# Conv gated MLP in FP32: eight gate tiles begun ahead and kept in DRAM, modulation in single pieces, last six down rows by halves

## Chip, cores and metric

One core of a Trainium2 chip. The metric is the device time of one execution in microseconds; several executions are timed and the median counts. One further execution is profiled. All rows of instructions below come from that one.

## What is computed

An encoder trunk of two layers on x of 1024 tokens by 1024 features, all in FP32. Each layer is a token mixer, which the change leaves alone, and a gated MLP with a convolution of three taps along the tokens. A vector c gives each layer six modulation vectors (shift, scale and gate of both halves).

```python
mod = (c_act @ w_mod[l] + b_mod[l])[:, None, :]
sh1, sc1, g1, sh2, sc2, g2 = jnp.split(mod, 6, axis=-1)
...
x = x + g1 * rms_norm(y, norm_g[l, 1])
h = rms_norm(x, norm_g[l, 2]) * (1 + sc2) + sh2
u = dwconv3(h @ w_up[l], ffn_conv[l])
ug, uv = jnp.split(u, 2, axis=-1)
y = (jax.nn.gelu(ug, approximate=True) * uv) @ w_down[l]
x = x + g2 * rms_norm(y, norm_g[l, 3])
```

D_FF is 2816, so w_up gives 22 tiles of 128 gate features and 22 of values, and w_down has 22 row blocks of 128.

## The kernel before

Features lie on the partitions and tokens along the free dimension, in two halves of 512. Every FP32 product is done as three matmuls on rounded parts, high by high, high by low, low by high; `split` (L110 and L111) makes a part pair from a loaded tile, the high part on ScalarE, the low part on GpSimd or VectorE.

**dense_up** makes one gate tile and its value tile per step t, 22 steps, from seven products of 512 by 512 blocks in place of eight, in the manner of Strassen, 84 matmuls of 128x512 each. `begin` (two quarters with the gate's own weight w1, 24 matmuls) needs token half 0 only; its result goes to u through ScalarE (L1218, L1222). `sums` loads both weights and makes three weight combinations on VectorE (L1238 to L1243); `head` (36 matmuls) and `tail` (24) use these with operands that need both token halves. Five `begin`s run ahead of all, kept in SBUF; the first head is mixed, its matmuls going through the operands one feature block at a time as these become ready. `gated` does the two convolutions (`conv3`, L919 and L921, 128x1024 each on VectorE), the gelu on ScalarE, the product (L1288) and the store to `actd` in DRAM.

**dense_down** walks over the 22 row blocks k. `whole` steps take two or four k, and for each of eight output tiles m run both token halves (48 matmuls per k) and add the result into y on VectorE (L1359, kept as `self.mark`). In layer 0 14 k go so; the last eight, in pairs, go by halves (`some`, 24 matmuls per k and half, adds L1366): first half 0 for all four pairs, then `end(HALVES[0])`, which does norm, residual and the next layer's modulated input for half 0 (lines L143 to L189, L446 to L452, L504, L505), then half 1 and its end. `load_half` is called directly ahead of each pair.

The modulation vectors that later stages need are made beside dense_down. `mod_sum` (L345) loads 16 weight blocks of 128x512; those of the first 512 outputs are multiplied and added up on VectorE (L365, L367), those of the second on ScalarE (L361) and GpSimd (L363). Each of the two series has one buffer. `background` calls it once per step, and a scheduler in the language places the instructions by the priorities that follow from the code's order; loads go on SyncE's queue in that order, and each waits at the head of the queue for its buffer.

Of the kernel before, what the change touches and what calls it, by code (L numbers as in the profile page):

```python
# [92 lines left out]
class Trunk:  # L93
# [251 lines left out]
    def mod_sum(self, l, j, room=None):  # L345

# [513 lines left out]
    def modulations(self):  # L860
# [3 lines left out]
        for j in (2, 4, 3):  # L864
            part = self.mod_sum(0, j, room)
# [50 lines left out]
    def conv3(self, o, t, cw):  # L916
        nc = self.nc
        n = o.shape[1]
        nc.vector.tensor_scalar(o, t[:, 0:n], cw(0), None, op0=ALU.mult)  # L919
# [160 lines left out]
    def mixer(self, l):  # L1080
        tc, nc = self.tc, self.nc
        with ExitStack() as e:
# [28 lines left out]
            self.uctx.close()  # L1111
            self.qlc, kls, rt, self.sc = self.open_shared(f"hmid{l}")
# [73 lines left out]
    def dense_up(self, l, early):  # L1186
# [12 lines left out]
        ahead = 5  # L1199
        with tc.tile_pool(name=f"ux{l}", bufs=4, reuse_waits="tile") as ux, \  # L1200
                tc.tile_pool(name=f"u2{l}", bufs=2, reuse_waits="tile") as u2p, \
                tc.tile_pool(name=f"a2{l}", bufs=1, reuse_waits="tile") as a2p:
            places = cycle(("tc", "tn", "ux", "ux", "ux", "ux"))
# [9 lines left out]
            def begin(w1, between=None):  # L1213

                u = u_tile()
# [3 lines left out]
                if between:  # L1219
                    between(u)  # L1220
                self.quarter(x, w1, 512, b21, False)
                nc.scalar.activation(u[:, c1], x, AF.Copy)  # L1222
                return u
# [24 lines left out]
            def rest(u, w2, w3, w4, uv):  # L1248

                state = {}  # L1250

                def head(u, mixed=False):
                    yb = self.psc.tile([128, 512], F32, name="psc", tag="psc")
                    zw = self.po.tile([128, 1024], F32, name="po", tag="po")
                    z, w = zw[:, 0:512], zw[:, 512:1024]
                    u2 = u2p.tile([128, 512], F32, name="u2", tag="u2")
                    jobs = ((yb, w2, 512, t2), (z, w2, 0, t1), (w, w4, 0, t4))
                    if mixed:
                        for i in range(4):
                            for ps, wx, at, xs in jobs:  # L1260
# [313 lines left out]
```

## Time and profile before

| | us |
|---|---|
| median of 3 runs | 3340.94 (3338.89 to 3341.43) |
| profiled execution | 3335.26 |
| its span | 3333.5 |
| TensorE busy in the span | 2895.6 (87%) |
| VectorE busy | 2380.3 (71%) |
| GpSimd busy | 1244.5 (37%) |
| ScalarE busy | 1167.9 (35%) |
| mean granted TensorE clock | 0.936 |

Times in rows are from the start of the span, which is 1.8 us shorter than the execution. In layer 0 the up projection begins at about 879 us, the down projection at 1374, and layer 1's input is ready at about 1810; in layer 1 the up projection begins at about 2561 and the down projection at 3054. The granted clock is a share of full speed: 1.00 is 2.4 GHz and 0.50 is 1.2 GHz.

### The profile page before, as it was taken

What the parts mean: (1) busy time and instruction counts of PE and PEld (TensorE: products, weight loads), DVE (VectorE), ACT (ScalarE), POOL (GpSimd) and SP (SyncE); (2) the same over time, 40 slices, a digit from 0 to 9 for tenths busy, and PEclk for the clock granted to TensorE, in tenths of its full rate; (3) what the DMA queues carried; (4) which work ended last, traced back from release to release, by engine and by line L of the source; (5) the groups of instructions that cost most, each with busy time, mean ns of one, the idle gap of its engine ahead of it and who ended that gap; (6) DMA issues with size and microseconds to landing.
All of it is one profiled execution on the core that took longest, in us unless ns stands there. A gap on an engine that the chain in (4) does not pass through costs nothing. (4 is left out here: it accounts for less than half of the span.)

```text
span 3333.5 us, 35440 instructions
## 1 busy us (share of the span) xinstructions
PE 2895.6 (87%) x13178; PEld 2296.9 (69%) x13178; DVE 2380.3 (71%) x3203; ACT 1167.9 (35%) x1698; POOL 1244.5 (37%) x853
## 2 busy tenths in 40 slices
PE   7888889988869999997358899889888689999997
PEld 3677667776557888776236787677766478887886
DVE  6686667796579898755485944676976698888456
ACT  4322433553432333322233333435544323333211
POOL 1221223224345545643353221333243454455431
PEclk8998999999979999998679999899999799999999
DMA  5235111012312222444332121101023122223423
GB/s 196 79 106 173 46 33 51 27 44 71 120 45 82 89 76 83 164 161 165 124 125 72 54 82 64 36 27 54 20 89 114 42 91 76 82 88 127 146 89 101
DMA packets 119513, 292.74 MB, mean 88 GB/s; under 512 B 13051, under 2 KB 31739, under 8 KB 119340
## 3 DMA queue, kind: packets, MB, share of 16 engines
q1 hardware_dynamic: 119340, 290.48, 26.4%
q8 instruction: 103, 1.69, 0.2%
q14 instruction: 70, 0.57, 0.1%
HBM read 238.09 MB, written 55.74 MB: 88 GB/s over the span
## 5 line engine op out<-in xcount | busy, mean ns | idle before, releaser
L111 POOL TENSOR_TENSOR wl<-raw,wh 128x1024 fp32r<-128x1024 f32 (+1 forms) x87 | 217.3, 2499 | 462.9 <-ACT wh L110 271.3
L521 PE MATMUL pj<-hh,wh 128*128 128x512 f32 x800 | 328.1, 410 | 12.9 <-DVE ql L570 8.5
L522 PE MATMUL pj<-hl,wh 128*128 128x512 f32 x800 | 322.0, 402 | 1.6 <-POOL hl L450 1.3
L525 PE MATMUL pj<-hh,wl 128*128 128x512 f32 x800 | 209.7, 401 | 0.0
L521 PEld LDWEIGHTS pj<-hh,wh 128*128 128x128 f32 x800 | 154.4, 193 | 53.2 <-issue 15.4
L522 PEld LDWEIGHTS pj<-hl,wh 128*128 128x128 f32 x800 | 154.3, 193 | 36.9 <-issue 2.2
L525 PEld LDWEIGHTS pj<-hh,wl 128*128 128x128 f32 x800 | 152.7, 192 | 36.4 <-issue 1.6
L681 PE MATMUL po<-s,v 128*96 128x128 f32 (+3 forms) x672 | 130.4, 355 | 42.0 <-ACT s L678 41.8
L681 PE MATMUL po<-hp,v 128*96 128x256 f32 x512 | 128.2, 407 | 29.4 <-ACT hp L678 29.0
L110 ACT ACTIVATE wh<-raw 128x1024 fp32r<-128x1024 f32 (+1 forms) x95 | 99.0, 1044 | 146.9 <-PE pj L522 75.6
L681 PEld LDWEIGHTS po<-s,v 128*96 128x96 f32 x672 | 97.9, 185 | 69.7 <-ACT s L678 54.6
L568 ACT ACTIVATE qh<-pj 64x512 fp32r<-64x512 f32 x128 | 107.1, 837 | 98.8 <-PE pj L525 53.3
L570 DVE TENSOR_TENSOR ql<-pj,qh 64x512 fp32r<-64x512 f32 x64 | 55.4, 866 | 115.5 <-ACT qh L568 114.8
L681 PEld LDWEIGHTS po<-hp,v 128*96 128x96 f32 x512 | 87.3, 175 | 64.7 <-ACT hp L678 36.1
L111 POOL TENSOR_TENSOR ul<-raw,uh 128x1024 fp32r<-128x1024 f32 x43 | 112.7, 2621 | 49.5 <-ACT uh L110 49.3
L552 DVE TENSOR_TENSOR ks<-pj,ks 64x512 fp32r<-64x512 f32 x56 | 51.2, 914 | 109.5 <-ACT ks L551 108.9
L921 DVE SCALAR_TENSOR_TENSOR tb<-u,par,tb 128x1024 f32<-128x1024 f32 x88 | 127.0, 1443 | 0.0
L363 POOL TENSOR_TENSOR mc<-mc,mr 128x512 f32<-128x512 f32 x49 | 69.7, 1422 | 152.9 <-ACT mr L361 152.9
L367 DVE SCALAR_TENSOR_TENSOR mc<-mr,cact,mc 128x512 f32<-128x512 f32 x49 | 52.9, 1079 | 100.9 <-DMA mr<-in_w_mod_dram 100.8
L668 PE MATMUL psc<-qh,ks 128*128 128x256 f32 (+2 forms) x272 | 88.5, 339 | 36.4 <-DVE s L796 15.3
L1359 DVE TENSOR_TENSOR y<-y,po 128x1024 f32<-128x1024 f32 x54 | 65.6, 1216 | 68.7 <-PE po L514 68.6
L921 DVE SCALAR_TENSOR_TENSOR ta<-u,par,ta 128x1024 f32<-128x1024 f32 x88 | 114.2, 1297 | 0.0
(562 smaller groups left out, 9126.1 us busy)
## 6 DMA issues: line engine op xcount, KB each, us to landing
mr<-in_w_mod_dram SPq DMA_DIRECT2D x144, 256.0 KB, 3.0
raw<-in_w_up_dram SPq DMA_DIRECT2D x54, 512.0 KB, 3.5
raw<-in_w_in_dram SPq DMA_DIRECT2D x52, 512.0 KB, 3.3
raw<-in_w_down_dram SPq DMA_DIRECT2D x52, 512.0 KB, 3.8
actd<-ta SPq DMA_DIRECT2D x44, 512.0 KB, 2.6
uh<-in_w_up_dram SPq DMA_DIRECT2D x26, 512.0 KB, 3.7
room<-in_w_mod_dram SPq DMA_DIRECT2D x48, 256.0 KB, 3.5
xd<-y SPq DMA_DIRECT2D x48, 256.0 KB, 2.4
```

The lines of the kernel that those rows point to most:

```text
L110: self.nc.scalar.activation(hi, src, AF.Copy)
L111: (eng or self.nc.gpsimd).tensor_sub(lo, src, hi.bitcast(F32))
L363: nc.gpsimd.tensor_add(acc, acc, w)
L521: nc.tensor.matmul(ps, wh[:, ks], self.hh[k][:, hs], start=k == 0, stop=False, skip_group_check=True)
L522: nc.tensor.matmul(ps, wh[:, ks], self.hl[k][:, hs], start=False, stop=False, skip_group_check=True)
L525: nc.tensor.matmul(ps, wl[:, ks], self.hh[k][:, hs], start=False, stop=k == KT - 1, skip_group_check=True)
L568: nc.scalar.activation(self.perm(qh[h][o:o + 64], r)[:, n * half:n * half + n, :], src, AF.Copy)
L570: nc.vector.tensor_sub(lo, src, own.bitcast(F32))
L668: nc.tensor.matmul(ps, ks[:, c], qh[:, q0:q1], start=first, stop=False, skip_group_check=True)
L681: nc.tensor.matmul(o[0:96, co], v(tt, h), s[:, cs], start=co.start // 512 not in seen, stop=False, skip_group_check=True)
L921: nc.vector.scalar_tensor_tensor(o, t[:, i:i + n], cw(i), o, op0=ALU.mult, op1=ALU.add)
L1359: self.mark = nc.vector.tensor_copy(d, p) if first else nc.vector.tensor_add(d, d, p)
```

## The change

Up projection, both layers: eight `begin`s in place of five run ahead; each u is stored to a DRAM tensor `kept` from ScalarE's queue and loaded again on SyncE's when its tile's turn comes. The first two tiles are done side by side in one mixed series of matmuls. The first term of each convolution moves from VectorE to ScalarE, and one of the adds at a tile's end from VectorE to GpSimd.

Modulation: 96 pieces (one load, one VectorE multiply-add) with two buffers, none on ScalarE or GpSimd; layer 0 places three behind each tile t of 8 and up, and one or two behind each output add of the down projection.

Down projection of layer 0: 16 k whole, six by halves; all loads of half 1 stand ahead of half 0's end.

```diff
-    def mod_sum(self, l, j, room=None):
+    def mod_pieces(self, l, j, room=None):
...
-                    w = self.mr.tile([128, 512], F32, name="mr", tag=f"mr{u}")
+                    w = self.mr.tile([128, 512], F32, name="mr", tag="mr")
...
-                if u and not room:
-                    nc.scalar.activation(w if k else acc, w, AF.Copy, scale=s)
-                    if k:
-                        nc.gpsimd.tensor_add(acc, acc, w)
-                elif k == 0:
+                if k == 0:
                     nc.vector.tensor_scalar(acc, w, s, None, op0=ALU.mult)
                 else:
                     nc.vector.scalar_tensor_tensor(acc, w, s, acc, op0=ALU.mult, op1=ALU.add)
+                yield
             accs.append(acc)
         return l, j, accs, 0
+    def modulate(self, jobs):
+        for l, j in jobs:
+            part = yield from self.mod_pieces(l, j)
+            self.mod_fold(part, self.mr.tile([128, 512], F32, name="mr", tag="mr"))
+            yield
+    def advance(self, n):
+        with self.tc.issue_after(self.mark.ins):
+            for _ in range(n):
+                next(self.pieces, None)
...
+        if scalar:
+            nc.scalar.activation(o, t[:, 0:n], AF.Copy, scale=cw(0))
+        else:
+            nc.vector.tensor_scalar(o, t[:, 0:n], cw(0), None, op0=ALU.mult)
...
-        ahead = 5
+        ahead = 8
+        kept = self.kept
...
+                def tail(p):
+                    u, uv = p.u, p.uv
+                    if p.x is None:
+                        self.quarter(p.y, p.w3, 0, t3, False)
+                        nc.vector.tensor_add(uv[:, c1], p.y, u[:, c2])
+                    else:
+                        nc.vector.tensor_add(uv[:, c1], p.x, p.u2)
+                    self.quarter(p.z, p.w3, 512, b22, False)
+                    nc.vector.tensor_add(u[:, c2], p.z, p.u2)
+                    nc.gpsimd.tensor_add(uv[:, c2], uv[:, c2], uv[:, c1])
+                    nc.vector.tensor_add(uv[:, c1], uv[:, c1], p.w)
+                    return u, uv
...
+            for t in range(ahead):
+                u = u_tile()
+                begin(u, early[t] if t < len(early) else self.up_weight(l, t))
+                nc.scalar.dma_start(kept[128 * t:128 * t + 128, :], u[:, 1:1025])
+            def kept_pair(t):
+                ws, u = sums(t, False), u_tile()
+                nc.sync.dma_start(u[:, 1:1025], kept[128 * t:128 * t + 128, :])
+                return Pair(u, ws)
+            two = [kept_pair(t) for t in range(2)]
+            jobs = []
+            for p in two:
+                p.x = self.pj.tile([128, 512], F32, name="pj", tag="pj")
+                jobs += [(p.y, p.w2, 512, t2), (p.z, p.w2, 0, t1), (p.x, p.w3, 0, t3)]
+            jobs.insert(2, two[0].p4)
...
+                if t >= ahead:
+                    self.advance(3)
...
             def whole(ops, first):
                 for m in range(8):
+                    if m:
+                        self.advance(1 if len(ops) < 4 else 2)
...
-                for j, ks in enumerate(final):
-                    some(load_half(ks, HALVES[0], room[j % 2]), HALVES[0], whole_half)
+                for ks in final:
+                    some(load_half(ks, HALVES[0], "ppp"), HALVES[0], part)
+                while next(self.pieces, self) is not self:
+                    pass
                 right.close()
+                rest = [load_half(ks, HALVES[1], names) for ks, names in zip(final, ("wwq", "qqq", "fff"))]
                 end(HALVES[0])()
-                for j, ks in enumerate(final):
-                    some(load_half(ks, HALVES[1], room[j % 2]), HALVES[1], whole_half)
+                for ops in rest:
+                    some(ops, HALVES[1], part)
                 end(HALVES[1])()
```

Three places show what moves. The first is SyncE's queue near the end of layer 0's down projection; `mr` are modulation weights, `raw<-in_w_down` weights of the down projection, `qh`, `ql`, `ph`, `pl` its other operand, `xd` the residual. Before:

```order
L501 DMA raw<-xd 128x2x512
L358 DMA mr<-in_w_mod_dram 128x512 x2
L1168 DMA qh<-actd 128x512
L1168 DMA ql<-actd 128x512
L358 DMA mr<-in_w_mod_dram 128x512 x28
L506 DMA xd<-y 128x512 x2
L116 DMA raw<-in_w_down_dram 128x1024
L506 DMA xd<-y 128x512 x6
L116 DMA raw<-in_w_down_dram 128x1024 x2
L501 DMA x<-xd 128x2x512 x2
```

Now (ten loads stand ahead of two whole operands, thirteen ahead of the last half pairs):

```order
L357 DMA mr<-in_w_mod_dram 128x512 x10
L1188 DMA ql<-actd 128x1024
L1188 DMA wl<-actd 128x1024
L116 DMA raw<-in_w_down_dram 128x1024
L1188 DMA qh<-actd 128x512
L1188 DMA ql<-actd 128x512
L357 DMA mr<-in_w_mod_dram 128x512 x13
L1188 DMA ph<-actd 128x512
L1188 DMA pl<-actd 128x512
L116 DMA raw<-in_w_down_dram 128x1024 x2
L357 DMA mr<-in_w_mod_dram 128x512
L1188 DMA ph<-actd 128x512
```

The row of 28 loads directly ahead of the residual's stores is gone; the loads stand earlier, in rows of 13 and fewer, with operand loads between them.

The second is VectorE (and GpSimd) in one steady tile of the up projection of layer 0. L1268 (now L1280) is the add behind the head, L1288 (L1308) the product, L1238 to L1243 (L1257 to L1262) the next weights' sums, L1275 to L1279 (L1293 to L1299) the adds behind the tail. VectorE before:

```order
L1268 TENSOR_TENSOR u_8132<-psc,u 128x512
L1288 TENSOR_TENSOR ta<-ta,tb 128x1024
L1238 TENSOR_TENSOR wl<-raw 128x512
L1239 TENSOR_TENSOR wl<-wl,wh 128x512
L1242 TENSOR_TENSOR raw<-wh,raw 128x512
L1243 TENSOR_TENSOR raw<-wh,wl 128x512
L1275 TENSOR_TENSOR u<-psc,u 128x512
L1278 TENSOR_TENSOR u<-u 128x512
L1277 TENSOR_TENSOR u<-po,u_8132 128x512
L1279 TENSOR_TENSOR u<-u,po 128x512
L919 TENSOR_SCALAR ta<-u,par 128x1024
L919 TENSOR_SCALAR tb<-u,par 128x1024
```

VectorE now (L360 and L362 are pieces):

```order
L1280 TENSOR_TENSOR u_7907<-psc,u 128x512
L1308 TENSOR_TENSOR ta<-ta,tb 128x1024
L360 TENSOR_SCALAR mc<-mr,cact 128x512
L1258 TENSOR_TENSOR ul<-ul,uh 128x512
L362 SCALAR_TENSOR_TENSOR mc<-mr,cact,mc 128x512
L1261 TENSOR_TENSOR raw<-uh,raw 128x512
L1262 TENSOR_TENSOR raw<-uh,ul 128x512
L362 SCALAR_TENSOR_TENSOR mc<-mr,cact,mc 128x512
L1293 TENSOR_TENSOR u<-psc,u 128x512
L1297 TENSOR_TENSOR u<-po,u_7907 128x512
L1299 TENSOR_TENSOR u<-u,po 128x512
L1257 TENSOR_TENSOR wl<-raw 128x512
```

GpSimd now, with the moved add L1298 at its place:

```order
L111 TENSOR_TENSOR vl<-raw,vh 128x512
L111 TENSOR_TENSOR ul<-ul,uh 128x1024
L111 TENSOR_TENSOR wl<-raw,wh 128x1024
L1298 TENSOR_TENSOR u<-u 128x512
```

The pieces stand behind the product and among the sums; both L919 and the add L1278 are gone from VectorE, and the moved add stands on GpSimd behind the splits of the next weights.

The third is ScalarE at the start of the up projection in layer 0, where the operands of token half 1 are prepared (`hx`, `hp`, `t4`, `y` are such operands, `u<-pj` the evacuations of begins). Before:

```order
L110 ACTIVATE t4_6553<-t_6538 128x512
L110 ACTIVATE y_6550<-x_6536 128x512
L110 ACTIVATE y_6556<-sq_6537 128x512
L1218 ACTIVATE u_6635<-pj_6638 128x512
L1218 ACTIVATE u_6671<-pj_6674 128x512
L110 ACTIVATE vh_6746<-raw_6740 128x512
L110 ACTIVATE uh_6744<-raw_6740 128x1024
L1222 ACTIVATE u_6635<-pj_6638 128x512
```

Now:

```order
L110 ACTIVATE t4_6560<-t_6545 128x512
L110 ACTIVATE y_6557<-x_6543 128x512
L110 ACTIVATE y_6563<-sq_6544 128x512
L1238 ACTIVATE u_6638<-pj_6647 128x512
L1238 ACTIVATE u_6675<-pj_6684 128x512
L110 ACTIVATE vh_6869<-raw_6863 128x512
L110 ACTIVATE uh_6826<-raw_6828 128x1024
L1242 ACTIVATE u_6638<-pj_6647 128x512
L1315 DMA kept_86<-u_6638 128x1024
```

The first evacuation of begin 3 (`u_6635`, now `u_6638`) stands behind the last prepared operand in both; the stores to `kept` are new.

## Rows read from the trace of the kernel before

**Rows 1.** Stretches; columns: us, busy (instructions) by engine, TensorE clock, DMA share, GB/s.

```profile
879.00:947.00 68.00, 39.10 (x111) 21.44 (x110) 49.54 (x71) 25.13 (x42) 30.93 (x19) 0.76 0.15 54
947.00:1080.00 133.00, 121.52 (x488) 97.02 (x487) 108.02 (x102) 37.67 (x48) 64.54 (x58) 0.93 0.24 79
1080.00:1374.00 294.00, 294.00 (x1278) 239.92 (x1277) 257.44 (x239) 96.10 (x123) 155.28 (x113) 1.00 0.24 84
1374.00:1608.00 234.00, 206.72 (x863) 164.34 (x861) 142.27 (x180) 66.70 (x82) 116.00 (x63) 0.95 0.52 175
1608.00:1690.00 82.00, 2.90 (x6) 0.88 (x4) 38.24 (x72) 13.58 (x20) 22.43 (x15) 0.52 0.31 101
3054.00:3314.00 260.00, 249.40 (x1168) 208.49 (x1167) 148.96 (x177) 58.44 (x72) 92.40 (x43) 0.98 0.34 117
```

**Rows 2.** TensorE's timeline: start us, us, line, operation [idle before it <-what ended that].

```profile
1608.47 0.39 PE L514 MATMUL pd<-ql 128*128 128x512 f32 x1
...
1690.36 0.80 PE L512 MATMUL pd<-qh,wh 128*128 128x512 f32 x1 [69.92 <-ACT wh L110]
```

**Rows 3.** SyncE's timeline, end of the down projection in layer 0.

```profile
1600.93 69.44 SPq L358 DMA_DIRECT2D mr<-in_w_mod_dram  x28
...
1684.83 0.45 SPq L116 DMA_DIRECT2D raw<-in_w_down_dram  x1
```

**Rows 4.** VectorE's line L367: what ended its idle time, us, times.

```profile
  DMA mr<-in_w_mod_dram: 100.8, 42
```

**Rows 5.** VectorE's timeline between the layers, the two half chains.

```profile
1680.07 0.71 DVE L143 STREAM_TRANSPOSE ta<-sm 128x512 f32<-128x512 f32 x1
...
1730.82 0.74 DVE L452 SCALAR_TENSOR_TENSOR hl<-tc,mod,hh 128x512 fp32r<-128x512 f32 x1
...
1757.41 0.69 DVE L1366 TENSOR_TENSOR y<-y,pd 128x512 f32<-128x512 f32 x1 [0.68 <-PE pd L514]
...
1767.71 0.71 DVE L143 STREAM_TRANSPOSE acc<-sm 128x512 f32<-128x512 f32 x1
...
1807.14 0.75 DVE L452 SCALAR_TENSOR_TENSOR hl<-t,mod,hh 128x512 fp32r<-128x512 f32 x1
```

**Rows 6.** TensorE's timeline, start of the up projection in layer 0.

```profile
929.74 0.80 PE L1263 MATMUL psc<-y,uh 128*128 128x512 f32 x1 [5.75 <-ACT y L110]
```

**Rows 7.** ScalarE's timeline, the same place.

```profile
945.11 0.58 ACT L1218 ACTIVATE u<-pj 128x512 f32<-128x512 f32 x1
```

**Rows 8.** VectorE's groups, 1080 to 1374 us: count | busy us, mean ns | idle.

```profile
L1278 DVE TENSOR_TENSOR u<-u 128x512 f32<-128x512 f32 x16 | 25.9, 1621 | 1.7
L919 DVE TENSOR_SCALAR tb<-u,par 128x1024 f32<-128x1024 f32 x15 | 24.0, 1601 | 0.0
...
L919 DVE TENSOR_SCALAR ta<-u,par 128x1024 f32<-128x1024 f32 x15 | 20.9, 1391 | 0.0
...
L1275 DVE TENSOR_TENSOR u<-psc,u 128x512 f32<-128x512 f32 x16 | 11.1, 692 | 23.3 <-PE psc L1184 23.3
```

**Rows 9.** Two of the page's costliest groups; columns as in rows 8.

```profile
L110 ACT ACTIVATE wh<-raw 128x1024 fp32r<-128x1024 f32 (+1 forms) x95 | 99.0, 1044 | 146.9 <-PE pj L522 75.6
...
L363 POOL TENSOR_TENSOR mc<-mc,mr 128x512 f32<-128x512 f32 x49 | 69.7, 1422 | 152.9 <-ACT mr L361 152.9
```

**Rows 10.** The page's DMA issues: count, KB each, us from issue to landing.

```profile
mr<-in_w_mod_dram SPq DMA_DIRECT2D x144, 256.0 KB, 3.0
raw<-in_w_up_dram SPq DMA_DIRECT2D x54, 512.0 KB, 3.5
...
actd<-ta SPq DMA_DIRECT2D x44, 512.0 KB, 2.6
```

**Rows 11.** VectorE's groups, 1374 to 1608 us; columns as in rows 8.

```profile
L367 DVE SCALAR_TENSOR_TENSOR mc<-mr,cact,mc 128x512 f32<-128x512 f32 x30 | 33.3, 1111 | 61.0 <-DMA mr<-in_w_mod_dram 60.9
```

**Rows 12.** VectorE's timeline, one steady tile of the up projection.

```profile
1161.81 0.68 DVE L1279 TENSOR_TENSOR u<-u,po 128x512 f32<-128x512 f32 x1
```

**Rows 13.** GpSimd's timeline, the same tile.

```profile
1159.33 2.85 POOL L111 TENSOR_TENSOR ul<-raw,uh 128x1024 fp32r<-128x1024 f32 x1
```

More of the change, by code (lines that the diff above doesn't have):

```diff
@@ L864, in modulations @@
         for j in (2, 4, 3):
-            part = self.mod_sum(0, j, room)
+            pieces = self.mod_pieces(0, j, room)
+            try:
+                while True:
+                    next(pieces)
+            except StopIteration as done:
+                part = done.value
             yield
@@ L1211, in u_tile, with begin @@
                 return u
[L1213 to L1215 removed]
+            def begin(u, w1, between=None):
                 x = self.pj.tile([128, 512], F32, name="pj", tag="pj")
@@ L1285, in gated @@
                     base = _P["fconv"] + l * 132 + m
-                    self.conv3(o, u, lambda i: self.par[:, base + 44 * i:base + 44 * i + 1])
+                    self.conv3(o, u, lambda i: self.par[:, base + 44 * i:base + 44 * i + 1], True)
                 nc.scalar.activation(cv[0], cv[0], AF.Gelu_apprx_tanh)
-                nc.vector.tensor_mul(cv[0], cv[0], cv[1])
+                self.mark = nc.vector.tensor_mul(cv[0], cv[0], cv[1])
                 nc.sync.dma_start(self.actd[128 * t:128 * t + 128, :], cv[0])
-            begun = [begin(early[t] if t < len(early) else self.up_weight(l, t)) for t in range(ahead)]
@@ L1292, in dense_up @@
-            for t in range(FT):
-                w1, w2, w3, w4 = sums(t, t >= ahead)
+            for t in range(ahead):
[6 more added lines that the diff above has]
+                return Pair(u, ws)
@@ new lines, in dense_up @@
+            two = [kept_pair(t) for t in range(2)]
[4 more added lines that the diff above has]
+            jobs.insert(2, two[0].p4)
+            for i in range(4):
+                for ps, w, at, xs in jobs:
+                    ks = slice(at + 128 * i, at + 128 * i + 128)
+                    for a, b in ((0, 0), (0, 1), (1, 0)):
+                        nc.tensor.matmul(ps, w[a][:, ks], xs[i][b], start=i == a == b == 0, stop=i == 3 and a == 1,
+                                         skip_group_check=True)
@@ L1294, in dense_up @@
+            self.quarter(*two[1].p4)
+            for p in two:
+                p.taken()
+            for t, p in enumerate(two):
+                gated(t, p.tail())
+            for t in range(2, FT):
                 if t < ahead:
-                    u, uv = begun[t], u_tile()
-                    head, tail = rest(u, w2, w3, w4, uv)
-                    head(u, t == 0)
-                else:
-                    uv = u_tile()
-                    head, tail = rest(None, w2, w3, w4, uv)
-                    u = begin(w1, head)
@@ L1368, in some @@
                         begun()
-            steps = [(2, "fwfw"), (4, "p" * 8), (4, "qqqqfwff")] + \
-                ([(2, "pppp")] * 4 if last else [(4, "p" * 8)])
-            mods = {0: (0, 5), 1: (1, 1), 2: (1, 0), 3: (1, 2), 4: (1, 4), 5: (1, 3)} if not last else {1: (1, 5)}
-            part, k = None, 0
-            def background(step):
-                if part:
-                    with tc.issue_after(self.mark.ins):
-                        self.mod_fold(part, self.mr.tile([128, 512], F32, name="mr", tag="mr0"))
-                if step in mods:
-                    return self.mod_sum(*mods[step])
-            step = 0
-            for n, names in steps:
-                ops = load(range(k, k + n), names)
-                whole(ops, k == 0)
-                part = background(step)
-                step += 1
-                if n == 4 and not last:
-                    part = background(step)
-                    step += 1
+            k = 0
+            for n, names in [(2, "fwfw"), (4, "p" * 8), (4, "qqqqfwff")] + \
+                    ([(2, "pppp")] * 4 if last else [(4, "p" * 8), (2, "wwqq")]):
+                whole(load(range(k, k + n), names), k == 0)
                 k += n
-            part = background(step)
             if last:
```

82 lines of the change are left out of this document (38 added, 44 removed).

## The prediction

> **What bounds the kernel now.** I first read the table of stretches [rows 1]. Between 1080 and 1374 us, the steady part of layer 0's up projection, TensorE is busy 294.00 of 294 us at clock 1.00, 1278 matmuls, so 294 / 1278 = 0.230 us each: there TensorE is the bound and a lighter VectorE brings nothing. Three other stretches are not like that. The start (879 to 947) has TensorE busy 39.10 of 68, the first tiles (947 to 1080) 121.52 of 133, and the down projection (1374 to 1608) 206.72 of 234, where layer 1's (3054 to 3314) has 249.40 of 260. The worst is 1608 to 1690: TensorE 2.90 of 82 us, and VectorE, ScalarE and GpSimd together less than that time too. So nothing computes there; something is waited for.
>
> TensorE's timeline [rows 2] says for what: after the last matmul of half 0 at 1608.47 (and two of the norm's) it sits 69.92 us until ScalarE has split a weight. SyncE's timeline [rows 3] says why the weight is late: 28 loads of the modulation weights hold the queue for 69.44 us, and the next w_down load is issued only behind them, at 1684.83. That is 2.48 us per load, as each pair of loads has two buffers in all and waits for the consumers of the pair before it; VectorE's L367 waits 100.8 us for such loads, 42 times [rows 4].
>
> **Part by part.** The sum is made against the profiled execution, 3335.26 us, which is 5.68 us under the median of 3340.94; gains are then taken from the median. About 0.2%, 6.7 us, is what a measurement can tell from no change.
>
> *Down projection, layer 0, to the end of half 0.* Before: from 1374 to 1608.47 = 234.5 us for 14 rows whole and half 0 of eight, 14 x 48 + 8 x 24 = 864 matmuls, which at 0.230 are 198.7; 35.8 us are waits. The change does 16 of 22 rows whole, then half 0 of six: 16 x 48 + 6 x 24 = 912 matmuls, 209.8 us (48 more before this point, 48 fewer behind it). In place of pairs that jam SyncE's queue, 56 pieces stand between the output adds, and the order shows w_down loads between them. For the waits left I take the 10.6 us that layer 1's stretch shows [rows 1]; below that 0, above it the old 35.8. Gain 234.5 - 220.4 = 14 us, bounds -11 and 25.
>
> *The boundary.* Before: from 1608.47 to the last split of half 1 at 1807.14 + 0.75 [rows 5], 199.4 us. The change loads half 1's operands ahead of the norm of half 0, so its 192 matmuls (44 us) run beside half 0's chain, and the modulation is drained before. What remains is VectorE's own chain: 1.0 us to the last add, from an add to the broadcast 1757.41 to 1767.71 = 10.3, from there to the last split of half 0 1680.07 to 1731.56 = 51.5 (10 adds of half 1 were among it; the change's order has 20, so 10 x 0.69 more), then half 1 from its last add 1757.41 to 1807.89 = 50.5. Sum 1.0 + 10.3 + 51.5 + 6.9 + 50.5 = 120.2, gain 199.4 - 120.1 = 79 us. VectorE's order in the change has the last add of half 1 just ahead of the last split of half 0, so the two chains do follow one another. Bounds: 20 us more if half 1's matmuls and adds fit into what are gaps of that chain and its squares overlap; 5 less for a further weight split that GpSimd does there.
>
> *Start of the up projection, both layers.* The eight begins do not fill the hole at 913 to 945. There TensorE waits for the last prepared operands, 5.75 us at a time [rows 6], and the evacuation of begin 3 runs on ScalarE at 945.11, behind the whole chain [rows 7]; in the change's order it still stands behind the chain. I count nothing for that part. Worse, 27 matmuls of the mixed pair that ran inside the wait now come behind it (6.2 us). Against it: the begins (120 matmuls, 27.6 us) then cover the weight sums of two pairs, and VectorE, 108.02 of 133 us busy in the first tiles [rows 1], loses per tile an add (1.62) and two first convolution terms (1.39 and 1.60) [rows 8]. ScalarE takes the terms at 1.04 each [rows 9]; it is busy 96.10 of 294. In the stretch 947 to 1080 488 matmuls are worth 112.2 us, 20.8 are lost. I take 10 as lost in the change (bounds 0 and 25): 20.8 - 10 - 6.2 = 5 us gain per layer. The store and return of u cost 2.6 + 3.5 = 6.1 us a tile [rows 10], on two queues, hidden by the begins (27.6 us) at first and by 60 matmuls (13.8 us) per tile later; uncovered they would cost 6.1 once per layer.
>
> *Steady up projection.* Period in layer 0: 84 x 0.230 = 19.3 us; VectorE 257.44 / 294 of it, 16.9. It loses 4.6 and takes three pieces of 1.11 [rows 11] and a share of the folds (I put 0.6): 16.2 in layer 0, 12.3 in layer 1. Its waits for TensorE, 23.3 us in 16 tiles for L1275 alone [rows 8], are slack. But the add that went to GpSimd stands there behind three weight splits, and VectorE's last add has to wait for it: at 1161.81 that add now starts [rows 12], while GpSimd is in a split from 1159.33 to 1162.18 [rows 13]; with the moved add at 1.42 [rows 9] it would start at 1163.6 or later, 2 us behind. 16.2 + 2 is still under 19.3. I take 5 us of loss in all for layer 0, none in layer 1 (bounds 0 and 40).
>
> *Layer 1's down projection* keeps its order but for pieces in place of pairs: 0 (bounds -5 and 5).
>
> Sum: 14 + 79 + (5 - 5) + 5 + 0 = 98 us. 3335 - 98 = 3237 for a profiled execution, and 3341 - 98 = **3243** for the median.
>
> **Rivals.**
> 1. *The wait moves to VectorE in the steady tiles.* For: the add on GpSimd, the third piece of a tile issued to SyncE behind a weight load, and 16.2 busy already. If these reach 6 us a tile, the period is 22.2, 2.9 x 14 = 40 us lost: 35 more than I took, 3278. Against: slack of 3.1 us, and loads of 3.0 us [rows 10] with three VectorE instructions between pieces.
> The Trainium skill (Perfetto Trace Analysis, Optimizing Scalar/DVE Operations) says that moving work from VectorE to GpSimd may not help, as the two share an SBUF port. The trace agrees in part [rows 8, 12] (L1278 takes 1.62 on average, L1279 0.68), and by that rule the moved add would bring VectorE nothing in the first tiles: up to 1.6 x 8 = 13 us per layer less, 3269 in all, inside this rival.
> 2. *Slower.* Each piece waits on VectorE for its own load, and the output add or tile add behind it waits too. The price is known: VectorE waited 100.8 us in 42 such instructions [rows 4], 2.4 each. In the up projection 16.2 + 7.2 = 23.4 a tile, 4.1 over the period, x 14 = 57. In the down projection 56 x (2.4 + 1.11) = 197 on top of 109 of other VectorE work there (142.27 [rows 1] less 33.3 [rows 11]) = 306, 86 over its 220. Together 143: 3243 + 143 = 3386, slower by 45. VectorE has about 1.0 us of slack per piece in both stages, so with 98 pieces the gain of 98 is gone from 2.0 us of wait per piece on. Against: two buffers in one tag, and at least two other VectorE instructions (an add of 1.2 and more) between most pieces; the waits of before came from a queue that had nothing else between pairs.
> 3. *The jam only shifts.* In the change's order of SyncE 13 modulation loads still stand ahead of the loads of the last half pairs; at 2.48 us each that is 32 us. If the matmuls queued there (two steps, about 35 us) do not cover it, 30 of the 98 go: 3273.
> 4. *More than I took.* No loss in the first tiles of either layer (20), no waits in the down projection (10), or the overlap at the boundary (20): 3243 - 50 = 3193 with all, 3213 with the first two.
>
> **Chances.** Forecast 0.58 (3220 to 3260), rival 1 0.13, rival 2 0.04, rival 3 0.08, rival 4 0.17. The range 3195 to 3278 takes in the forecast, rival 1 to its price, rival 3 and all but the far end of rival 4; outside are rival 2, sums of 1 and 3, and that far end, some 0.15. Faster: all but rival 2 and a share of sums of mishaps (two rivals at once), 0.94; within 0.2% 0.02; slower 0.04.
>
> **What would show it.** No idle of TensorE above 15 us between the last matmul of half 0 and those of half 1; then a stretch of about 120 us with VectorE near full; the down projection at 95% busy; the first wait in the up projection still 30 us long at clock 0.50; the steady tiles at 19.3 us. I am wrong if TensorE waits for VectorE in every steady tile (rival 1), if the pieces show a wait of 2 us or more each for their loads (rival 2), or if half 1's first matmul still waits for a weight (rival 3).

## The result and the profile after

The changed kernel takes 3297.28 us (median of 4 runs, 3292.14 to 3301.45) where the kernel before takes 3339.91 on the same chip: a ratio of 0.9873 (0.9856 to 0.989). The forecast was 3243, its range 3195 to 3278. The gain is 43 us, not 98. The profiled execution took 3296.84, 38.4 under the one of before.

The stretches of the changed kernel; columns as in [rows 1].

```profile
875.00:945.00 70.00, 33.46 (x103) 19.57 (x101) 48.02 (x68) 29.12 (x48) 32.74 (x23) 0.75 0.25 85
945.00:1005.00 60.00, 55.90 (x215) 43.96 (x216) 13.06 (x15) 14.87 (x21) 20.91 (x27) 0.90 0.35 123
1005.00:1120.00 115.00, 97.31 (x395) 77.33 (x395) 100.60 (x87) 46.33 (x50) 62.48 (x56) 0.92 0.35 119
1200.00:1414.00 214.00, 198.27 (x839) 157.29 (x838) 167.20 (x183) 85.96 (x102) 105.03 (x86) 0.99 0.33 109
1414.00:1652.00 238.00, 216.48 (x915) 174.40 (x914) 184.47 (x215) 55.83 (x62) 95.08 (x43) 0.97 0.52 174
1652.00:1754.00 102.00, 82.82 (x294) 55.13 (x293) 81.73 (x138) 38.27 (x59) 35.10 (x26) 0.93 0.31 105
```

The last row was the hole of [rows 1, 2]: TensorE is now busy 82.82 of 102 us there. The steady tiles, 294.00 of 294 before, are at 198.27 of 214.

The table has the length of each stage, from the starts of its first and last matmul and, in layer 0's up projection (up 0), of the product of the ninth tile and of the last. "Boundary" is from the end of half 0 in layer 0's down projection (down 0) to the first matmul of layer 1's up projection (up 1); all of layer 1's token mixer lies in it. One profiled execution each; two of them differ by a few us without cause. Runs e1 to e12 are the experiments below.

| | up 0 to ninth tile | ninth to last | down 0 to end of half 0 | boundary | up 1 | down 1 |
|---|---|---|---|---|---|---|
| before | 253.7 | 251.9 | 234.6 | 953.0 | 492.1 | 260.3 |
| after | 275.2 | 277.9 | 237.7 | 857.0 | 502.5 | 263.6 |
| e1_add_dve | 270.9 | 276.0 | 236.7 | 860.6 | 487.1 | 261.6 |
| e2_conv_dve | 280.6 | 291.4 | 237.2 | 860.1 | 511.5 | 265.3 |
| e3_pieces_down | 270.8 | 266.2 | 261.6 | 864.8 | 502.5 | 265.6 |
| e4_old_up | 251.4 | 254.1 | 255.0 | 863.2 | 492.1 | 261.0 |
| e5_room | 251.5 | 265.3 | 261.0 | 863.4 | 501.2 | 264.7 |
| e6_add_room | 247.3 | 255.5 | 258.3 | 868.0 | 487.6 | 262.0 |
| e7_even | 247.2 | 255.6 | 254.6 | 868.8 | 487.3 | 264.0 |
| e8_three | 245.9 | 255.8 | 239.4 | 866.8 | 488.1 | 265.2 |
| e9_split2 | 247.9 | 275.9 | 229.8 | 855.5 | 487.3 | 261.8 |
| e10_split3 | 247.2 | 273.5 | 232.2 | 855.0 | 487.7 | 262.1 |
| e11_mixed | 246.0 | 255.3 | 249.6 | 863.6 | 487.5 | 261.2 |
| e12_fill | 248.1 | 274.2 | 235.6 | 855.4 | 487.3 | 264.3 |

The boundary gave 96 us: 100 up to the last split of half 1, less 4 by which layer 1's mixer got longer. The up projections took 21.5 and 26.0 back in layer 0 (of which its last tile returns 3), 10.4 in layer 1; the down projections lost 3 each. Another 4 us were gained ahead of up 0; their cause is not known.

TensorE's timeline of the changed kernel, start of up 0 (in timelines here and below: start, us, engine, line, operation, then the idle time before it), and ScalarE's at that place:

```profile
944.93 0.79 PE L1200 MATMUL pj<-hp,uh 128*128 128x512 f32 x1 [33.05 <-ACT u L1238]
```

```profile
944.30 0.58 ACT L1238 ACTIVATE u<-pj 128x512 f32<-128x512 f32 x1
```

The waits of [rows 6], with the mixed pair's matmuls between them, have become one of 33.05 us, in which TensorE does nothing: begin 3's evacuation is where it was [rows 7], and all else stands behind it. VectorE then idles as well, 13.06 busy of 60 us in the second stretch. First it waits for the last matmuls of begins, to make the sums of the next weights (L1257), then for the mixed pair's matmuls (L1280). SyncE's largest wait and VectorE's, 920 to 1005 us (in lists of waits: who, for whom, us in total, times, longest):

```profile
SPq L1249 <- POOL ul L111: 48.8, 2, 45.0
DVE u L1280 <- PE psc L1333: 13.8, 1, 13.8
DVE ul L1257 <- PE pj L1204: 11.5, 1, 11.5
DVE wl L1257 <- PE pj L1204: 9.1, 1, 9.1
```

The time is lost behind this long wait and not in it. Up to its end both kernels needed about the same (69.8 and 67.9 us). From there to the product of the ninth tile, the changed kernel and then the one before; columns as in [rows 1]:

```profile
945.00:1150.40 205.40, 183.61 (x741) 146.03 (x742) 135.37 (x123) 73.78 (x87) 97.55 (x98) 0.93 0.33 113
947.00:1132.80 185.80, 174.31 (x717) 140.15 (x716) 154.03 (x145) 54.39 (x69) 92.95 (x80) 0.95 0.24 80
```

At 0.230 us the 741 matmuls are worth 170.4 us, so 35.0 are lost; before, 717 were worth 164.9, and 20.9 were lost.

VectorE's waits in the steady tiles, 1200 to 1414 us, ten tiles, and TensorE's two largest:

```profile
DVE u L1299 <- POOL u L1298: 26.8, 10, 4.7
DVE raw L1262 <- POOL vl L111: 18.8, 6, 3.6
DVE mc L362 <- DMA mr<-in_w_mod_dram: 3.0, 3, 1.9
```

```profile
PE po L1200 <- ACT u L1281: 9.0, 5, 2.9
PE psc L1200 <- DVE u L1280: 4.1, 3, 3.4
```

The same line L1299 in layer 1, 2720 to 2990 us, columns as in [rows 8]:

```profile
L1299 DVE TENSOR_TENSOR u<-u,po 128x512 f32<-128x512 f32 x13 | 9.0, 690 | 49.5 <-POOL u L1298 49.5
```

VectorE is busy 167.20 / 10 = 16.7 us a tile, and waits (26.8 + 18.8 + 3.0) / 10 = 4.9 more, for GpSimd nearly all of it; together 21.6, about the period of 21.4. Before, its waits in such tiles were for TensorE [rows 8], and TensorE had none.

The page's group of the pieces, both layers, and VectorE's wait for their loads in the down projection of layer 0, 1414 to 1652:

```profile
L362 DVE SCALAR_TENSOR_TENSOR mc<-mr,cact,mc 128x512 f32<-128x512 f32 x98 | 107.1, 1092 | 17.6 <-DMA mr<-in_w_mod_dram 17.1
```

```profile
DVE mc L362 <- DMA mr<-in_w_mod_dram: 12.9, 15, 1.3
```

The 100.8 us of [rows 4] are down to 17.1. At the boundary, half 1's first matmul follows half 0's last at once:

```profile
1651.98 0.40 PE L523 MATMUL pd<-pl 128*128 128x512 f32 x1
1652.21 0.41 PE L521 MATMUL pd<-qh,wh 128*128 128x512 f32 x1
```

### The profile page after: what moved, and what is told of

Its sections match the earlier page's. It is cut to its first block, busy times and chain, and to the rows that moved or that the text cites. A ratio compares the mean times of both kernels' runs of the same rounds, so it can differ in the third digit from the quotient of the medians.

```text
span 3295.0 us, 35545 instructions
## 1 busy us (share of the span) xinstructions
PE 2898.2 (88%) x13178; PEld 2295.2 (70%) x13178; DVE 2293.4 (70%) x3120; ACT 1219.3 (37%) x1726; POOL 1208.9 (37%) x877
## 5 line engine op out<-in xcount | busy, mean ns | idle before, releaser
L111 POOL TENSOR_TENSOR wl<-raw,wh 128x1024 fp32r<-128x1024 f32 (+2 forms) x82 | 201.4, 2457 | 467.5 <-ACT wh L110 277.1
L111 POOL TENSOR_TENSOR ul<-raw,uh 128x1024 fp32r<-128x1024 f32 x51 | 130.2, 2556 | 93.9 <-ACT uh L110 93.7
L110 ACT ACTIVATE wh<-raw 128x1024 fp32r<-128x1024 f32 (+2 forms) x90 | 94.1, 1046 | 167.9 <-PE pj L531 76.5
L577 ACT ACTIVATE qh<-pj 64x512 fp32r<-64x512 f32 x128 | 107.1, 837 | 97.0 <-PE pj L534 51.5
L938 DVE SCALAR_TENSOR_TENSOR ta<-u,par,ta 128x1024 f32<-128x1024 f32 x88 | 135.8, 1543 | 3.4 <-ACT ta L934 3.2
L938 DVE SCALAR_TENSOR_TENSOR tb<-u,par,tb 128x1024 f32<-128x1024 f32 x88 | 136.7, 1553 | 0.3
L1410 DVE TENSOR_TENSOR y<-y,po 128x1024 f32<-128x1024 f32 x60 | 73.0, 1217 | 87.6 <-PE po L523 87.6
L111 POOL TENSOR_TENSOR pl<-raw,ph 128x1024 fp32r<-128x1024 f32 x26 | 67.2, 2591 | 147.5 <-ACT ph L110 104.4
L362 DVE SCALAR_TENSOR_TENSOR mc<-mr,cact,mc 128x512 f32<-128x512 f32 x98 | 107.1, 1092 | 17.6 <-DMA mr<-in_w_mod_dram 17.1
```

The lines of the kernel that those rows point to most:

```text
L110: self.nc.scalar.activation(hi, src, AF.Copy)
L111: (eng or self.nc.gpsimd).tensor_sub(lo, src, hi.bitcast(F32))
L577: nc.scalar.activation(self.perm(qh[h][o:o + 64], r)[:, n * half:n * half + n, :], src, AF.Copy)
L938: nc.vector.scalar_tensor_tensor(o, t[:, i:i + n], cw(i), o, op0=ALU.mult, op1=ALU.add)
L1410: self.mark = nc.vector.tensor_copy(d, p) if first else nc.vector.tensor_add(d, d, p)
```

## Experiments

The theory after the first reading: three things cost in the up projection, the add on GpSimd, the pieces, and something at the start of layer 0. Rivals: VectorE's time alone, or late weights. Ratios are to the kernel before on the same chip, with 95% intervals; the changed kernel has 0.9873. The expectations count 102 pieces in layer 0: the 96 pieces and a last step (a fold) for each of the six vectors.

**e1_add_dve**

```diff
-                    nc.gpsimd.tensor_add(uv[:, c2], uv[:, c2], uv[:, c1])
+                    nc.vector.tensor_add(uv[:, c2], uv[:, c2], uv[:, c1])
```

> The changed kernel with one line undone: the add that went from VectorE to GpSimd is back on VectorE. Theory (the add stands behind weight splits on GpSimd and VectorE's last add of a tile waits for it, 26.8 us in ten tiles): the steady tiles of layer 1 return from about 20.3 to 19.3 us and layer 1's up projection from 502 to about 492 us; in layer 0 the tiles fall from 21.3 to 19.5-20.5. Total 20 to 35 us less than the changed kernel, 3262 to 3277. Rival (the pieces and ScalarE's convolution terms are the load, the wait only fills time that is lost anyway): layer 1 stays at 500 or more, total within 8 us of 3297.

Measured: 3275.41 us, 0.9787 (0.9769 to 0.9805), inside the theory's range. Up 1 falls by 15.4 to 487.1, 5 under the old kernel's. VectorE's group, 2720 to 2990 us:

```profile
L1298 DVE TENSOR_TENSOR u<-u 128x512 f32<-128x512 f32 x14 | 14.5, 1039 | 1.5
```

The add costs VectorE 1.04 us; waiting for it on GpSimd had cost 49.5 / 13 = 3.8. In layer 0 only 8.8 us come back in the whole of up 0 (530.1 for 538.9), and a tile takes 276.0 / 13 = 21.2 us, not the 19.5 to 20.5 that were expected: the pieces are still there (e6 is without them).

**e2_conv_dve**

```diff
-                    self.conv3(o, u, lambda i: self.par[:, base + 44 * i:base + 44 * i + 1], True)
+                    self.conv3(o, u, lambda i: self.par[:, base + 44 * i:base + 44 * i + 1])
```

> The changed kernel with one line undone: the first convolution terms are back on VectorE. Theory (VectorE waits for GpSimd, and has little time over beside that wait): two more VectorE operations a tile (1.4 and 1.6 us) stand on the same chain, so the tiles get longer, by 1 to 3 us: 3310 to 3370. Rival (ScalarE's terms lie in the chain and hold it up): 10 us or more less than 3297.

Measured: 3325.41 us, 0.9932 (0.9907 to 0.9957). Slower than the changed kernel, as the theory said: the terms on ScalarE are worth 14.5 us in up 0 and 9.0 in up 1.

**e3_pieces_down**

```diff
-                if t >= ahead:
-                    self.advance(3)
...
-                        self.advance(1 if len(ops) < 4 else 2)
+                        self.advance(2 if len(ops) < 4 else 4)
```

> The changed kernel with no modulation pieces in the up projection; the down projection takes two or four behind each output add in place of one or two. The written order now has begins 3 to 5 of layer 0 among the preparing of half 1, as layer 1 has it. Theory: layer 0's start becomes layer 1's (16 us less), its steady tiles too (21.3 to 20.3, 13 us less), and the down projection pays 0 to 20 for 46 more pieces: 3268 to 3290. Rival (the down projection cannot take them: 102 loads in about 190 us): its waits grow past 30 us and the total is 3297 or more.

Measured: 3314.31 us, 0.9903 (0.9882 to 0.9924). A miss; the rival's time came. The steady tiles gained 11.7, but the pieces cost 23.9 where they went, where VectorE's L362 waits 41.9 us for loads, and 7.8 at the boundary. Nor did the long wait at the start of up 0 go, as the expectation had assumed:

```profile
949.06 0.79 PE L1200 MATMUL pj<-hp,uh 128*128 128x512 f32 x1 [33.08 <-ACT u L1238]
```

**e4_old_up.** The up projection of before (`dense_up` whole), all pieces in the down projection as in e3, their pools opened there as in e5.

```diff
-        ahead = 8
-        kept = self.kept
+        ahead = 5
...
-            two = [kept_pair(t) for t in range(2)]
...
```

> The up projection as it was before the change (five begins, all in memory, one mixed pair, convolution and adds on VectorE, no pieces), with the changed down projection and boundary, which take all pieces as in e3. Theory (the down projection and the boundary give 93 us, as forecast, and the up projection takes 40 to 55 of them back): 3340 - 93 = 3247, plus 0 to 20 for the extra pieces: 3247 to 3267, clearly under the changed kernel. Rival (some of the 93 comes from the new up projection): over 3285.

Measured: 3272.56 us, 0.9776 (0.9753 to 0.9799). A little above what was expected, but under the changed kernel by 0.0097, 32 us. The boundary keeps 90 us of its gain beside the old up projection, though the down projection, now with all pieces, is 20 longer than before; the new up projection was a net loss.

**e5_room.** As e3, and the pools of the modulation opened in the down projection.

```diff
-            if l == 0:
-                self.mods = ExitStack()
-                self.mc, self.mr = (p(n, 2, self.mods, side="right") for n in ("mc", "mr"))
...
-            if last:
-                self.mc, self.mr = (right.enter_context(tc.tile_pool(name=f"{n}{l}", bufs=2, reuse_waits="tile",
+            self.mc, self.mr = (right.enter_context(tc.tile_pool(name=f"{n}{l}", bufs=2, reuse_waits="tile",
```

> The kernel with all pieces in the down projection, and with the pools of the modulation opened there too and not during the mixer, so that u's buffers no longer lie where memory comes free late. In the order, begins 3 to 5 then stand between the steps of VectorE's and ScalarE's operand chain in layer 0. Theory (the pools' memory holds the begins back): the one 33 us wait of TensorE at the start of layer 0's up projection breaks up into waits under 10 us, and 12 to 18 us go against the kernel with the same pieces and the early pools, ratio 0.990 there: about 0.985 to 0.987, 3292 to 3299 where before is 3341. Rival (the operand chain itself, or the weight buffers that eight begins hold, set the start): the wait moves behind the begins and the time stays within 5 us of 0.990.

Measured: 3296.46 us, 0.9854 (0.984 to 0.9869). TensorE's timeline at the start of up 0:

```profile
927.82 0.80 PE L1197 MATMUL pj<-hp,wh 128*128 128x512 f32 x1 [6.25 <-ACT u L1235]
945.46 0.80 PE L1197 MATMUL pj<-hx,uh 128*128 128x512 f32 x1 [7.21 <-ACT u L1239]
```

33.08 have become 6.25 and 7.21, and the first nine tiles take 251.5 in place of 270.8. Nothing but the pools' place differs from e3, so that place is the cause of the one long wait and of these 19 us. (The old kernel had no such pools, and its begin 3 stood behind the chain too; there the mixed pair's matmuls ran amid the chain instead.) That it works through u's buffers, which then lie where memory comes free late, fits the order (in e5 begins 3 to 5 stand between the chain's steps); no view shows addresses.

**e6_add_room.** e5 and e1 together.

> As the kernel before it, and the add on GpSimd (L1298 of the changed kernel) back on VectorE. Theory (that add's wait costs some 0.6 to 1 us in every steady tile of both layers, as the run with only the add put back showed): 20 to 28 us less than without, about 0.977 to 0.980; both up projections near 487 us, 5 under the old kernel's. Rival (with no pieces in the up projection, VectorE has room enough to wait): under 10 us.

Measured: 3266.86 us, 0.9761 (0.9745 to 0.9778). With no pieces in the way, the add gives 4.2 and 9.8 us in up 0 and 13.6 in up 1.

**e7_even** and **e8_three.** e6, with the pieces spread evenly; then a third load buffer.

```diff
-                        self.advance(2 if len(ops) < 4 else 4)
+                        self.advance(1 if len(ops) < 4 else 3)
...
                     self.mark = nc.vector.tensor_add(y[m][:, hs], y[m][:, hs], ps)
+                    self.advance(1)
```

> As the kernel before it, with the pieces spread evenly over the down projection: three behind an output add of a four-row step, one behind an add of a two-row step, one behind each add of half 0's pairs, in place of four and two and none. Theory A (four pieces of 1.1 and an add of 1.2 us make 5.6 us of VectorE per output tile, where 24 matmuls give TensorE 5.5; only the crowding costs): the stretch to the end of half 0 falls from about 255 to 245 us or less, 10 to 15 us less in all, about 0.973 to 0.975. Theory B (each piece costs its 0.3 to 0.5 us wherever it stands, by its wait for its load): within 4 us of the kernel before it.

```diff
-            self.mc, self.mr = (right.enter_context(tc.tile_pool(name=f"{n}{l}", bufs=2, reuse_waits="tile",
-                                                                 side="right")) for n in ("mc", "mr"))
+            self.mc, self.mr = (right.enter_context(tc.tile_pool(name=f"{n}{l}", bufs=b, reuse_waits="tile",
+                                                                 side="right")) for n, b in (("mc", 2), ("mr", 3)))
```

> As the kernel before it, with three buffers for the loads of the modulation in place of two. If a piece's price is the wait for its load (40 us in 32 waits in the run with all pieces in the down projection), VectorE's waits for modulation loads at least halve and 5 to 10 us go; if SyncE's queue, held by a load that waits for its buffer, is what delays the weights, about the same; if the price is VectorE's own time, nothing (within 3 us).

Measured: 3262.57 us, 0.9753 (0.9738 to 0.9767), and 3254.08 us, 0.972 (0.9706 to 0.9735). Spreading alone hardly helps: 4.3 us, and 3.7 of the stretch where theory A wanted 10 to 15. VectorE's waits in the down projection, e7 first, 1365 to 1615 us, e8 1367 to 1615:

```profile
DVE mc L362 <- DMA mr<-in_w_mod_dram: 44.5, 40, 2.6
```

```profile
DVE mc L362 <- DMA mr<-in_w_mod_dram: 10.4, 13, 2.8
```

The third buffer takes 34 us of waits away and 15.2 us off the stretch. There most of a piece's price was the wait for its load.

**e9_split2**, **e10_split3**, **e12_fill.** e8, with 34 of 102 pieces back in up 0, in pools opened inside `dense_up`: two buffers, three buffers, and three with the pieces ahead of the last weight sum.

```diff
+                tc.tile_pool(name=f"mcu{l}", bufs=2, reuse_waits="tile") as mcu, \
+                tc.tile_pool(name=f"mru{l}", bufs=2, reuse_waits="tile") as mru:
...
+                if t >= ahead:
+                    self.advance(3)
```

> The best kernel so far (add on VectorE, the modulation's pools not open during the mixer, three load buffers; 0.972) with 34 of the 102 pieces back in layer 0's up projection, three behind each tile from the ninth, in pools of their own with TWO load buffers that displace nothing; the other 68 in the down projection with three buffers, one or two behind an add. Theory (a piece costs the wait for its load where two buffers serve it, about 0.48 us of TensorE in the up projection): the up projection 487 + 34 x 0.48 = 503 us, the down projection to the end of half 0 some 5 to 8 us shorter than 239, together about 8 to 12 us slower than that kernel: 0.974 to 0.976. Rival (the pieces cost in the changed kernel only because it had no room otherwise; here they are hidden): up projection under 492, ratio 0.969 to 0.971.

> The same with THREE load buffers in the up projection too. Theory (the wait for the load is the price): the up projection of layer 0 falls from about 503 to 487 to 493 us, the time to 0.969 to 0.972. Rival A (VectorE's own time for the pieces is the price): as with two buffers, within 3 us. Rival B (the loads on SyncE's queue, each waiting for its buffer ahead of a weight load, are the price): as with two buffers or a little less, and TensorE then waits for late weight sums.

```diff
-                nc.vector.tensor_sub(a21, a11, a21)
+                self.mark = nc.vector.tensor_sub(a21, a11, a21)
+                if t > ahead:
+                    self.advance(3)
                 nc.vector.tensor_sub(a22, a12, s2)
```

> As the run with three load buffers in the up projection (0.973; up projection of layer 0 506 us, 20 over the one without pieces), with the three pieces of a tile moved on VectorE from behind the product to a place directly ahead of the last weight sum (L1262 of the changed kernel), which waits 20 to 24 us in 6 or 7 of the tiles for GpSimd's split of another weight. Theory (VectorE is full in these tiles, 200 us busy of 240 and the rest mostly that wait; the price of a piece is VectorE's time, and it is free where it fills the wait): the up projection of layer 0 falls to 490 to 497 us, the time by 9 to 16 us, 0.968 to 0.970. Rival A (the wait is slack and the chain that binds runs through VectorE's sums to the splits of the next weights): a piece ahead of the sum delays these just as much, up projection 504 to 510, 0.972 to 0.974. Rival B (a piece's load waits at the head of SyncE's queue ahead of the weights wherever it stands): the same as A in time, with the wait for the loads seen on VectorE.

Measured: 3246.62 us, 0.9728 (0.9713 to 0.9743); 3248.83 us, 0.9731 (0.9714 to 0.9747); 3250.79 us, 0.9715 (0.9702 to 0.9728). All within the interval of e8. The 34 pieces cost 18 to 20 us in up 0 each time and give about 4 to 10 back in the down projection and 11 at the boundary. Neither the third buffer nor the other place changed their price. The steady tiles, 1130 to 1370 us, of e8 (no pieces), e10 and e12, one row of each; columns as in [rows 1]:

```profile
1130.00:1370.00 240.00, 240.00 (x1044) 195.88 (x1044) 182.59 (x170) 103.60 (x125) 118.57 (x94) 1.00 0.25 85
```

```profile
1130.00:1370.00 240.00, 229.62 (x964) 184.43 (x963) 200.18 (x216) 95.15 (x115) 114.01 (x91) 0.97 0.33 110
```

```profile
1130.00:1370.00 240.00, 225.24 (x960) 180.34 (x959) 212.85 (x216) 93.39 (x113) 113.25 (x91) 0.99 0.33 107
```

And the wait that e12 meant to fill, e10 first:

```profile
DVE raw L1262 <- POOL vl L111: 20.1, 6, 3.6
```

```profile
DVE raw L1264 <- POOL vl L111: 9.1, 4, 4.3
```

The wait (L1262, in e12 L1264) fell by 11 us, and the same 216 VectorE instructions took 12.67 us more; 10.4 of these are the 26 pieces themselves (mean 943 ns in e10, 1341 in e12). So the theories of e10 and e12 fall, and e9's rival too; e9's theory had the price of a piece nearly right, but neither its reason nor the 11 us at the boundary. In time, both rivals of e10 and of e12 fit. What tells them apart is what ScalarE's splits of the weights wait for in these tiles. Two such waits of e8, then of e10:

```profile
ACT uh L110 <- DMA wh<-in_w_up_dram: 11.2, 3, 4.1
ACT uh L110 <- DVE wl L1255: 11.9, 4, 3.4
```

```profile
ACT uh L110 <- DMA wh<-in_w_up_dram: 11.1, 2, 6.1
ACT uh L110 <- DVE wl L1258: 20.8, 5, 5.3
```

All such waits for weight loads come to 30.0 us in e8 and 28.8 in e10, so the weights are not later, and VectorE has no wait for a piece's load among its own; the rivals B fall. Those for VectorE's weight sums come to 58.5 in e8, 80.8 in e10 and 80.9 in e12. The pieces hold up these sums wherever they stand, by VectorE's own time: rival A of e10, and more exactly that of e12.

**e11_mixed.** e8, half of each job's pieces as before the change:

```diff
+                if u and not room:
+                    nc.scalar.activation(w if k else acc, w, AF.Copy, scale=s)
+                    if k:
+                        nc.gpsimd.tensor_add(acc, acc, w)
-                if k == 0:
+                elif k == 0:
```

> The best kernel so far (all pieces in the down projection, three buffers, spread evenly; 0.972) with the second half of each job's pieces multiplied on ScalarE and added on GpSimd, as the old kernel did. Its TensorE waited 29 us in the down projection for VectorE's output adds. Theory (VectorE, some 102 pieces of 1.1 us there, is what is left): half of these waits go, the stretch to the end of half 0 falls from 239 to 225 to 232 us, ratio 0.968 to 0.970. Rival (the adds stand in GpSimd's queue ahead of the splits of the weights, as the moved add did in the up projection): the stretch grows, 0.973 to 0.98.

Measured: 3250.89 us, 0.9737 (0.9716 to 0.9758). In time not to be told from e8, but the stretch grew from 239.4 to 249.6 as the rival said, if not by the rival's way: VectorE waits 41.0 us for the high parts of the down projection's weights and operands, which ScalarE makes, the engine that now multiplies too; in e8 it waits 5.2 us for them. GpSimd's adds wait for ScalarE as well, and GpSimd is busy 141 of 248 us where e8 has 96. VectorE's two largest such waits, 1367 to 1615 us:

```profile
DVE ql L111 <- ACT qh L110: 10.9, 2, 10.3
DVE ql L111 <- ACT ql L110: 10.4, 2, 7.4
```

## Why the prediction was wrong

*Boundary: right in kind, 21 us too small.* Forecast 120.2 us from half 0's last matmul to the last split of half 1; it is 1651.98 to 1751.20, 99.2. 14.4 of the 21 are one step: from the broadcast to the last split of half 0, forecast at 51.5 + 6.9, took 1660.17 to 1704.15 = 44.0. In the old trace instructions of that chain ran at up to four times their usual length (others of line L446 took 0.74 us), and the sum had taken these over. One of them, with what GpSimd was doing at that moment:

```profile
1712.49 2.84 DVE L446 SCALAR_TENSOR_TENSOR tn<-y,gm,ta 128x512 f32<-128x512 f32 x1
1712.13 2.65 POOL L111 TENSOR_TENSOR wl<-raw,wh 128x1024 fp32r<-128x1024 f32 x1 [2.46 <-ACT wh L110]
```

What rival 4 priced at 20, as gaps to be filled, so came in part as such instructions getting short again. Two readings were wrong without harm to the sum. Half 1 has 144 matmuls (33 us), not 192 (44). And the old hole at the boundary was not the 28 loads alone: between their end at 1670.37 and the weight's load at 1684.83 SyncE's queue stood before two stores of the residual (13.6 us of it waiting for GpSimd's add L505); the change puts the load ahead of these too.

*Down projection, layer 0: sized wrong, inside its bounds.* +14 was forecast, -3 measured. In place of the 10.6 us of waits taken over from layer 1 there are 237.7 - 209.8 = 27.9, with pieces on VectorE and two load buffers. VectorE waits 12.9 us for the pieces' loads there. That they are behind most of the excess is argued from e8, where the third buffer gave 15.2 us with all pieces in this stretch; no run gave the changed kernel itself a third buffer. In the columns of the table the two terms were forecast at 93 and gave 93: that is luck, 21 us more at the boundary against 17 less here and 4 less in layer 1's mixer.

*Start of the up projection: the step that failed first.* That the begins "then cover the weight sums of two pairs" did not hold in layer 0. The text saw that begin 3 would still stand behind the chain, and it priced the mixed pair's matmuls that now come behind the long wait rightly (27 at 6.2 us; there are 24 more, 5.5 us). But it took 10 us as lost behind that wait, and 35.0 were: a weight load waited 45.0 us for a buffer that a split on GpSimd had yet to free, and VectorE waited 20.6 us for the begins' last matmuls before it could make weight sums. Forecast +5, measured -21.5. The remedy was outside the lines that the text looked at: with the new pools opened later, begins run amid the chain, and 19.3 us come back (e5). In layer 1, which has no such pools in the mixer, the start lost 1.4. With room, and the add on VectorE, the start gains 6 to 8, which is near the +5.

*Steady up projection: the mechanism named, the size missed; this is rival 1.* "16.2 + 2 is still under 19.3" had VectorE's work right (16.7 a tile), and the wait at L1299 nearly (2.7). It left out the second wait for GpSimd, L1262's 1.9 a tile; in the trace before, VectorE's waits in these tiles were for TensorE, and this one did not show. With both, VectorE's work and waits come to 21.6, over the 19.3. Forecast -5 and 0, measured -26.0 and -10. TensorE waits for ScalarE more than for VectorE there, and not in every tile, so rival 1's sign came only in part. The causes overlap: from 277.9 us the add alone gives 1.9 (e1), the pieces alone 11.7 (e3), both 22.4 (e6, with the pools moved). Rival 1's "third piece behind a weight load" is not what costs: 3.0 us of waits for loads in ten tiles.

The Trainium skill (Perfetto Trace Analysis, Optimizing Scalar/DVE Operations) says that moving work from VectorE to GpSimd may not help, as they share an SBUF read port. The result agrees: the move back gained 0.0086 of 3344 us, 29 us (e1). In the rows the loss is first of all VectorE waiting for GpSimd's turn (49.5 us in layer 1); no run separates from it what the port costs. That the two engines hold each other up inside instructions, the traces show (last section).

*Rivals 2 and 3* did not come: 17.1 us of waits for pieces' loads in 98, where rival 2 needed 2 us each, and no hole at the boundary. *Layer 1's down projection*: 0 forecast, -3.3 measured, within its bounds.

The best versions measured, e8 to e12, are at 0.972 to 0.974 and can't be told apart. They keep the boundary and ScalarE's terms, undo the add's move and the pools' place, and have most or all pieces in the down projection. What stays open: how the 0.5 to 0.6 us that a piece costs in up 0 divides. VectorE is not busy for over 25 us of 240, so it is not short of time as such. The pieces hold up the weight sums (e10, e12), and some pieces take 1.7 to 2.9 us in place of 0.74 (last section); no run removed the GpSimd splits beside them.

## What to carry over

A cheap instruction moved to another engine costs its place in that engine's queue: find what stands ahead of it there, and who waits behind the waiter. A mean is a poor price where the same instruction takes 0.7 us or 2.8, by what runs beside it. Sum an engine's busy time and its waits per tile, and ask of each wait whether it is slack or will stay when the tile changes. When new pools open early, look at where the scheduler puts work that has nothing to do with them. And a load in a series wants as many buffers as cover its flight: two to three was worth 15 us in the down projection, and nothing in the up projection.

## What the runs showed of the hardware

Some VectorE instructions, all of whose tensors lie in SBUF (L362, L446, L1298 are those looked at), get longer when they start while GpSimd is in a split. A piece (L362) in e10 that starts inside a split, the split, and the next piece, which starts with none under way:

```profile
1186.91 1.78 DVE L362 SCALAR_TENSOR_TENSOR mc<-mr,cact,mc 128x512 f32<-128x512 f32 x1
1186.00 2.14 POOL L111 TENSOR_TENSOR vl<-raw,vh 128x512 fp32r<-128x512 f32 x1
1189.22 0.74 DVE L362 SCALAR_TENSOR_TENSOR mc<-mr,cact,mc 128x512 f32<-128x512 f32 x1
```

The first ends 0.55 us behind the split. In the traces of the changed kernel, e8, e9, e10 and e12 together, 135 instructions of line L362 start while GpSimd is in a split or another instruction on two tensors, and 126 of them end 0.54 to 0.56 us behind it; of the 565 others 563 take 0.76 us or less. The L446 shown above does the same. L1298 on VectorE takes 1.04 us on average in layer 1 in e1: 11 of 14 take 0.70, the three that start inside a split 1.84 to 2.66. L1299, which has one operand in PSUM, is not held up; here it is in e1, inside a split:

```profile
2743.70 0.68 DVE L1299 TENSOR_TENSOR u<-u,po 128x512 f32<-128x512 f32 x1
2742.54 2.43 POOL L111 TENSOR_TENSOR wl<-raw,wh 128x1024 fp32r<-128x1024 f32 x1 [1.96 <-ACT wh L110]
```

This is most of why the same 216 VectorE instructions took 200.18 us in e10 and 212.85 in e12: in e12 ten of the 26 pieces take 1.66 us or more, in e10 five. So filling VectorE's wait for GpSimd with pieces did not shorten the stretch (273.5 us in e10, 274.2 in e12).
